# Seven products instead of eight for a sixth pair of the output projection, and an order of pairs of its own for the first block of every stage

## The chip, the cores and the metric

The kernel runs on one core of one Trainium2 chip. The metric is the device time of one execution in microseconds. The kernel before takes 2615.23 us, the median of three runs (2615.0 to 2615.27). Engines are named as in the profile: PE multiplies matrices, PEld loads the stationary operand, DVE, ACT and POOL work on elements, SP only issues DMAs.

## The reference

Two layers of an encoder trunk over 256 tokens of width 4096, everything in float32:

```
for l in range(2):
    h = rmsnorm(x, norm_w[l])
    proj = h @ w_in[l]                      # 4096 -> 11264
    aq, ak, av, ag, rq, rk, rv, rg = split(proj)
    a_out = silu(ag) * gqa_attention(rope(rmsnorm(aq)), rope(rmsnorm(ak)), av)
    r_out = silu(rg) * rmsnorm(bidirectional_retention(rope(rq), rope(rk), rv))
    x = x + concat(a_out, r_out) @ w_out[l] # 4096 -> 4096
return rmsnorm(x, final_norm)
```

Nearly all arithmetic is in the two projections of each layer.

## The kernel before

**Four stages.** Stage 0 is `w_in` of layer 0 (11 blocks of 1024 output columns), stage 1 `w_out` of layer 0 (4 blocks), stages 2 and 3 the same for layer 1. A block multiplies the transposed activations (256 tokens) by 1024 columns of weights. The 4096 input features are cut into 32 tiles of 128, and two neighbouring tiles make a *pair*; a block runs over pairs 0 to 15.

**Three passes for one product.** Weights and activations are split into a high part (rounded to the matmul format) and a low part (the rest), and a product is high by high, high by low, low by high: three matmuls of 512 columns (two at L1559, one at L1569). Pairs 1 and 0 of the very first block take the raw float32 values instead (L1553).

**Eights and sevens.** A pair is a 2 by 2 by 2 problem: two token halves, two feature tiles, two column halves. Done plainly it is eight products (`EIGHT_PRODUCTS`), done in Strassen's way seven (`SEVEN_PRODUCTS`). The table `SEVENS` names the pairs that take seven in each stage, five in every stage of the kernel before. The price of a seven is paid elsewhere. An eight has two weight pages (A and B, 128x1024): each is a load `wraw`, a cast on ACT to `whi`, and a subtraction on DVE to `wlo`. A seven has the same two loads but three and a half pages: A, T and U (128x1024) and half a page B (128x512, `bhi` and `blo`). T and U are sums of the loaded weights, made on DVE in `wsum` by three additions, and need casts and subtractions of their own. On the activations' side a seven needs five sums `xf`, split into `x7h` and `x7l`; an eight only `x8h` and `x8l`.

**Banks.** Eight PSUM banks M1 to M8 hold a block's sums. M1, M5, M7 and M6 serve sevens alone, so they open with the block's first seven and close with its last; outside that window they are lent to attention and retention, whose matmuls stand at L1040 to L1042. At a block's end `combine` adds the banks into `ca` and `cb`. Where DVE is behind, ACT copies a bank to `out` first.

**What sets the order.** The instructions are issued by a planner that runs in the program while it is built: it keeps clocks for PE, DVE and ACT with its own costs (`STEP_V`, `STEP_S`, `LANDING` and others), and between two products it puts in a step of a waiting *task* (rotary, attention, retention, norms, splitting of the next stage's operands) if the weights that PE needs next leave room. The order that comes out is fixed on every engine. Five buffers `whi`, five `wlo`, two each of `bhi` and `blo`, two `wsum` and six `wraw` limit how far DVE and ACT run ahead of PE. Loads of weights are issued by SP; stores, fetches and accumulating DMAs by POOL.

**Between stages.** Activations for the next stage go out transposed to `next_dram` in six chunks of two pairs, are fetched again into `full`, and split; the last two chunks are handed over in SBUF. The residual is added by an accumulating DMA into `ca` and `cb` (L1667 in the last stage).

`GROUPS` cuts the pairs at each seven: the pages of the eights that follow a seven are put between its pages (`TURNS`). Only the first block of all has an order of its own:

```
SEVENS = ((3, 4, 6, 10, 11), (4, 6, 10, 11, 12), (3, 4, 6, 10, 11), (4, 6, 10, 11, 12))
SPREAD = (4, 5, 9, 10, 13)
FIRST_ORDER = [1, 0] + [_p for _p in range(2, NP) if _p not in SEVENS[0]]
...
        for g in FIRST_GROUPS if first_order else GROUPS[stage]:
```

A page can also be made *far*, in a page of the common pool and outside the ring of five: ACT casts it to `fhi`, writes its negative to `flo`, and an accumulating DMA on POOL's queue adds the weights to `flo`, so that DVE has no part in it. `FARS` names such pages; it is empty in the kernel before.

Of the kernel before, what the change touches and what calls it, by code (L numbers as in the profile page):

```python
# [14 lines left out]
ALU = mybir.AluOpType  # L15
# [24 lines left out]
FAR = 1  # L40

STRICT = 9
RELIEF = 0.6
AHEAD = 5
SPARE = 2

HALVES = 2

STEP_V = 1.2
STEP_S = 1.5  # L50

V_FIXED = 0.1
# [3 lines left out]
PASS = 0.3  # L56

LANDING = 9.5
STORE = 5.0
FETCH = 13.0  # L60
FAR_LANDING = 9.0
MARGIN = 0.5

RUSH = 2.5

EARLY = 1.3

ADD_AHEAD = 3.0

NEED = {"ak": 4, "ag": 3, "rk": 5, "rg": 4}  # L70

PE_REST = 1.2

TIGHT_A = 2
TIGHT_B = 9

AT_ONCE = 3

WARM = 20

SPLITS = 1

START = 2

SEVENS = ((3, 4, 6, 10, 11), (4, 6, 10, 11, 12), (3, 4, 6, 10, 11), (4, 6, 10, 11, 12))

EVER = sorted(set(_p for _s in SEVENS for _p in _s))
EIGHTS = [_p for _p in range(NP) if _p not in EVER]
# [9 lines left out]

HOLD = 4

NEAR = 40

LATE = 10

FARS = ((), (), (), ())


AQ, AK, AV, AG, RQ, RK, RVO, RG = 0, 2048, 2560, 3072, 5120, 6144, 7168, 9216
# [65 lines left out]
GROUPS = [  # L174
    ([tuple(range(_s[0]))] if _s[0] else []) + [tuple(range(_a, _b)) for _a, _b in zip(_s, _s[1:] + (NP,))] for _s in SEVENS
]
SPREAD = (4, 5, 9, 10, 13)
FIRST_ORDER = [1, 0] + [_p for _p in range(2, NP) if _p not in SEVENS[0]]
for _i, _p in zip(SPREAD, SEVENS[0]):
    FIRST_ORDER.insert(_i, _p)  # L180
FIRST_GROUPS = []
for _p in FIRST_ORDER:
    if _p in SEVENS[0] or not FIRST_GROUPS:
        FIRST_GROUPS.append(())
    FIRST_GROUPS[-1] += (_p,)
SHARED = ("M1", "M5", "M7", "M6")


# [34 lines left out]
EASY = ("M7",)  # L223


BANK_REST = 0.8
APART = 0.0

TOGETHER = 4
# [52 lines left out]
def hybrid_encoder(  # L282
# [134 lines left out]
    class Weights:  # L417


        def __init__(self):  # L420
            self.pages = []
            for l in range(DEPTH):
                for w, n in ((w_in, N_IN), (w_out, N_OUT2)):
                    for b in range(n):
                        stage = 2 * l + (w is w_out)
                        start = (l, b) == (0, 0) and w is w_in
                        for g in FIRST_GROUPS if start else GROUPS[stage]:
# [337 lines left out]
    def split_operand(c, stage, rest=0.0):  # L765
        v, full[c] = full[c], None
        for k in range(2):
            p = 2 * c + k
            whole = None
            if stage == 0:  # L770
                whole = v.rearrange("p (k i n) -> p k i n", k=2, i=2)[:, k]
                w = v.rearrange("p (k i m a t) -> p k m i a t", k=2, i=2, m=MT, t=BLK)[:, k]
            else:
                w = v.rearrange("p (a m i t) -> p m i a t", a=4, m=MT, t=BLK)[:, :, 2 * k : 2 * k + 2]
            waiting.append(Lane(split_pair(p, w, whole, stage)))
            waiting[-1].pair, waiting[-1].ready = p, now.t + rest
        if stage == 0:
            waiting.sort(key=lambda v: (v.pair in NATIVE and not c, FIRST_ORDER.index(v.pair)))

    def split_late():  # L780
        split_operand(*late.pop(0))
# [77 lines left out]
    force = [False]  # L859

    def take_bank():

# [73 lines left out]
    def running():  # L936
# [4 lines left out]
            one.append(rest)  # L941
        return one

    def advance():

        clear()
# [17 lines left out]
    def tick():  # L964

        weights.low_parts()
# [456 lines left out]
    def lead(stage):  # L1423

        return 8 * SEVENS[stage][0]

    def block(after_pair, phase, then, first_order=False, order=LAST_ORDER, last=None, hurried=False):

# [5 lines left out]
        flat = []  # L1434
        stage = phase - 1
        rush[0] = RUSH if hurried else 0.0
        for g in FIRST_GROUPS if first_order else GROUPS[stage]:
            for slot in slots_of(g, stage, first_order):
                flat += slot
        want[0] = 2  # L1440
# [58 lines left out]
            return a  # L1499

        opens = max(final[b] for b in SHARED)
        after = lead(then - 1) if then else 0

        def end_product(n, name, p, index, k, h):
            g = pages[p, k]
# [70 lines left out]
    def combine(bank, acc, c):  # L1576
# [15 lines left out]
        elif bank in ("M8", "M3", "M2", "M4"):  # L1592
            to = {"M8": cb[:, 1, :], "M3": cb[:, 0, :], "M2": ca[:, 0, :], "M4": ca[:, 1, :]}[bank]
            v = acc[bank]
            if not last_block[0] and ve.until - max(ac.until, now.t) > RELIEF and held[0] + pledged() < PAGES:
                v = page([P, NB], "out")
                ac.copy(v, acc[bank])
                drop()
            ve.tensor_add(to, to, v)

# [250 lines left out]
    for l, L in enumerate(layers):  # L1851
        for bi, (one, _) in enumerate(BLOCKS):
# [10 lines left out]
            c = block(after, 2 * l + 1, 2 * l + 1 + (bi == N_IN - 1), start)  # L1863
            ready = (lambda i=one[1], L=L: i in L.weights) if one[0] == "rg" else None
            tasks.append(Lane(in_task(L, *one, c), need=NEED[one[0]], own=2, gate=ready))
            if one[0] == "ag":
                users.update((v, l, one[1]) for v in "sv")
                tasks.append(Lane(attention_scores(L, one[1]), need=6, gate=lambda g=one[1], L=L: g in L.rs and now.t >= L.kept and near(LATE)))
# [5 lines left out]
        for n in range(N_OUT2):  # L1874
# [19 lines left out]
            else:  # L1894
                if final:
                    turning.append(Turn(2 * l + 2))
                c = block(after, 2 * l + 2, 2 * l + 2 + (n == N_OUT2 - 1), hurried=n == 0)
                tasks.append(Lane(out_tasks(l, n, c), need=4, own=2))


_INS = [
# [46 lines left out]
```

## Time and profile before

| what | before |
|---|---|
| median of 3 runs | 2615.23 us |
| the profiled execution | 2615.02 us |
| its span | 2613.2 us |
| instructions in the span | 33651 |
| HBM read, written | 564.20 MB, 44.04 MB |
| DMA engines, mean busy share, by stage | 0.72, 0.72, 0.71, 0.64 |

The span is that of the program's instructions; 1.8 us of the execution lie outside it. Matmuls are pipelined: the profile gives each of 512 columns about 389 ns, but the next starts long before that, so what one costs is read from the distance of starts. A busy PE is then no proof that PE is at its peak; that has to be seen from starts and waits.

### The profile page before, as it was taken

What the parts mean: (1) busy time and instruction counts of PE and PEld (TensorE: products, weight loads), DVE (VectorE), ACT (ScalarE), POOL (GpSimd) and SP (SyncE); (2) the same over time, 40 slices, a digit from 0 to 9 for tenths busy, and PEclk for the clock granted to TensorE, in tenths of its full rate; (3) what the DMA queues carried; (4) which work ended last, traced back from release to release, by engine and by line L of the source; (5) the groups of instructions that cost most, each with busy time, mean ns of one, the idle gap of its engine ahead of it and who ended that gap; (6) DMA issues with size and microseconds to landing.
All of it is one profiled execution on the core that took longest, in us unless ns stands there. A gap on an engine that the chain in (4) does not pass through costs nothing.

```text
span 2613.2 us, 33651 instructions
## 1 busy us (share of the span) xinstructions
PE 2599.5 (99%) x11650; PEld 2152.7 (82%) x11650; DVE 2283.5 (87%) x2715; ACT 1636.4 (63%) x2376; POOL 238.6 (9%) x368
## 2 busy tenths in 40 slices
PE   9999999999999999999999999999999999999998
PEld 7888888888888888888888888888888888888886
DVE  7998988998888998778998889988988798988777
ACT  7765766666555687555785566675665557765454
POOL 0010211111001000110001101210100010000000
PEclk9999999999999999999999999999999999999999
DMA  7876867876666666786777768777765676667774
GB/s 281 297 246 234 274 224 246 278 230 225 205 212 213 238 209 205 238 274 223 260 228 233 223 233 274 244 232 263 253 225 179 223 232 226 198 205 221 231 243 167
DMA packets 180667, 610.47 MB, mean 234 GB/s; under 512 B 21904, under 2 KB 28560, under 8 KB 180496
## 3 DMA queue, kind: packets, MB, share of 16 engines
q1 hardware_dynamic: 147040, 520.17, 59.4%
q0 software_dynamic: 32736, 87.05, 11.1%
q8 instruction: 91, 1.49, 0.2%
q10 hardware_dynamic: 720, 1.10, 0.1%
q14 instruction: 80, 0.66, 0.1%
HBM read 564.20 MB, written 44.04 MB: 233 GB/s over the span
## 4 chain that ended last, share of the span: by engine, by line
PE 97%; DVE 1%; issue 1%; ACT 1%; DMA 1%; SPq 0%; POOLq 0%; DVEq 0%; POOL 0%; ACTq 0%
PE M L1559 62%; PE M L1569 31%; PE M L1042 1%; PE M L1041 1%; PE M L1040 1%; PE M L1553 0%; DVE wlo L267 0%; DMA wraw<-in_w_in 0%; DMA whole<-in_w_in 0%; ACT whi L267 0%; DVE wsum L267 0%; DVE cb L267 0%; ACT ca L267 0%; DVE ca L267 0%; DVE x7l L267 0%
## 5 line engine op out<-in xcount | busy, mean ns | idle before, releaser
L267 ACT CAST whi<-wraw 128x1024 fp32r<-128x1024 f32 x806 | 835.5, 1047 | 555.8 <-PE M L1559 490.5
L267 DVE TENSOR_TENSOR wlo<-wraw,whi 128x1024 fp32r<-128x1024 f32 x806 | 965.2, 1214 | 129.5 <-ACT whi L267 127.5
L1559 PE MATMUL M<-whi,x8h 128*128 128x512 f32 x2368 | 922.1, 389 | 0.0
L1559 PE MATMUL M<-whi,x8l 128*128 128x512 f32 x2368 | 921.7, 389 | 0.0
L1569 PE MATMUL M<-wlo,x8h 128*128 128x512 f32 x2368 | 679.3, 389 | 0.0
L1559 PEld LDWEIGHTS M<-whi,x8h 128*128 128x128 f32 x2368 | 444.6, 188 | 92.1 <-issue 0.2
L1559 PEld LDWEIGHTS M<-whi,x8l 128*128 128x128 f32 x2368 | 444.6, 188 | 92.0 <-issue 0.2
L1569 PEld LDWEIGHTS M<-wlo,x8h 128*128 128x128 f32 x2368 | 442.8, 188 | 90.8
L267 ACT CAST whi<-wsum 128x1024 fp32r<-128x1024 f32 x300 | 315.5, 1052 | 227.9 <-DVE wsum L267 115.3
L1559 PE MATMUL M<-whi,x7h 128*128 128x512 f32 x1140 | 443.6, 389 | 0.0
L1559 PE MATMUL M<-whi,x7l 128*128 128x512 f32 x1140 | 443.5, 389 | 0.0
L267 DVE TENSOR_TENSOR wlo<-wsum,whi 128x1024 fp32r<-128x1024 f32 x300 | 365.5, 1218 | 27.0 <-ACT whi L267 26.6
L1569 PE MATMUL M<-wlo,x7h 128*128 128x512 f32 x1140 | 341.3, 389 | 0.3 <-DVE wlo L267 0.3
L1569 PEld LDWEIGHTS M<-wlo,x7h 128*128 128x128 f32 x1140 | 213.8, 188 | 45.2 <-DVE wlo L267 0.7
L1559 PEld LDWEIGHTS M<-whi,x7h 128*128 128x128 f32 x1140 | 214.0, 188 | 44.9 <-issue 0.4
L1559 PEld LDWEIGHTS M<-whi,x7l 128*128 128x128 f32 x1140 | 214.0, 188 | 44.4
L267 DVE TENSOR_TENSOR wsum<-wraw 128x1024 f32<-128x1024 f32 x150 | 182.4, 1216 | 1.5 <-DMA wraw<-in_w_in 1.5
L267 DVE TENSOR_TENSOR wsum<-wsum,wraw 128x512 f32<-128x512 f32 x150 | 103.8, 692 | 5.2
L267 DVE TENSOR_TENSOR wsum<-wraw,wsum 128x512 f32<-128x512 f32 x150 | 102.5, 684 | 0.6
L267 DVE TENSOR_TENSOR blo<-wraw,bhi 128x512 fp32r<-128x512 f32 x150 | 102.7, 685 | 0.0
L267 ACT CAST bhi<-wraw 128x512 fp32r<-128x512 f32 x150 | 92.3, 615 | 0.0
L267 DVE TENSOR_TENSOR cb<-cb,M 128x512 f32<-128x512 f32 x85 | 58.0, 682 | 37.5 <-PE M L1569 37.4
(223 smaller groups left out, 1876.6 us busy)
## 6 DMA issues: line engine op xcount, KB each, us to landing
wraw<-in_w_in SPq DMA_DIRECT2D x700, 512.0 KB, 4.5
wraw<-in_w_out SPq DMA_DIRECT2D x256, 512.0 KB, 4.2
full<-next_dram POOLq DMA_DIRECT2D x18, 512.0 KB, 7.4
kv<-kv_dram POOLq DMA_DIRECT2D x16, 512.0 KB, 7.0
p_dram<-room POOLq DMA_DIRECT2D x64, 128.0 KB, 3.6
pT<-p_dram POOLq DMA_DIRECT2D x16, 512.0 KB, 8.6
next_dram<-room POOLq DMA_DIRECT2D x40, 128.0 KB, 4.9
x<-in_x SPq DMA_DIRECT2D x8, 512.0 KB, 6.6
```

The costliest lines, as they stand in the source:

```text
L267: return call(out, *args, **kwargs)
L1040: nc.tensor.matmul(out, a[0], b[0], start=start, stop=False)
L1041: nc.tensor.matmul(out, a[0], b[1], start=False, stop=False)
L1042: nc.tensor.matmul(out, a[1], b[0], start=False, stop=stop)
L1559: nc.tensor.matmul(acc[name], a[i], g.hi[h], start=m == first[name] and not i, stop=False)
L1569: nc.tensor.matmul(acc[name], a, g.lo[h], start=False, stop=m == final[name])
```

## The change

- `SEVENS`: in both `w_out` stages pairs 3, 4, 6, 10, 11 and 13 take seven products (before 4, 6, 10, 11 and 12). The `w_in` stages keep 3, 4, 6, 10 and 11. So pairs 3 and 13 are new among the sevens of `w_out`, and pair 12 is an eight again.
- The first block of every stage has an order of its own, by the tables `SPREAD` to `SPREAD3`. Where the first seven stands in it (`LEADS`) tells the planner how long the four shared banks stay free.
- `FARS` names pair 5 in the last stage: its page B is made far in three of that stage's blocks.
- The planner's numbers: among others `STEP_V` from 1.2 to 2.0 and `PE_REST` from 1.2 to 1.5 (more room is asked for before a task's step is put in), `AT_ONCE` from 3 to 2 tasks, `START` from 2 to 1, `RELIEF` from 0.6 to 1.0.
- `combine` could give an addition to an accumulating DMA, if DVE were late by more than `ADDED`, which is 99.

```
-RELIEF = 0.6
-AHEAD = 5
-SPARE = 2
+RELIEF = 1.0
+ADDED = 99
+AHEAD = 6
+SPARE = 3
...
-STEP_V = 1.2
+STEP_V = 2.0
...
-AT_ONCE = 3
+AT_ONCE = 2
...
-START = 2
+START = 1
-SEVENS = ((3, 4, 6, 10, 11), (4, 6, 10, 11, 12), (3, 4, 6, 10, 11), (4, 6, 10, 11, 12))
+SEVENS = ((3, 4, 6, 10, 11), (3, 4, 6, 10, 11, 13), (3, 4, 6, 10, 11), (3, 4, 6, 10, 11, 13))
...
-FARS = ((), (), (), ())
+FARS = ((), (), (), (5,))
...
+SPREAD = (3, 4, 7, 11, 13)
+SPREAD1 = (3, 6, 8, 10, 11, 13)
+SPREAD2 = (3, 4, 7, 9, 11)
+SPREAD3 = (6, 7, 9, 11, 13, 14)
+def opening_order(stage):
+    spread = (SPREAD, SPREAD1, SPREAD2, SPREAD3)[stage]
+    spread = spread if len(spread) == len(SEVENS[stage]) else SEVENS[stage]
+    order = [_p for _p in ([1, 0] if stage == 0 else [0, 1]) + list(range(2, NP)) if _p not in SEVENS[stage]]
+    for i, p in zip(spread, SEVENS[stage]):
+        order.insert(i, p)
+    return order
...
+FIRST_ORDER = [opening_order(_i) for _i in range(4)]
+FIRST_GROUPS = [grouped(_o, _i) for _i, _o in enumerate(FIRST_ORDER)]
+LEADS = [8 * next(_i for _i, _p in enumerate(_o) if _p in SEVENS[_s]) for _s, _o in enumerate(FIRST_ORDER)]
...
-        for g in FIRST_GROUPS if first_order else GROUPS[stage]:
+        for g in FIRST_GROUPS[stage] if opening else GROUPS[stage]:
...
-        after = lead(then - 1) if then else 0
+        after = 0 if not then else lead(then - 1) if then == phase else LEADS[then - 1]
...
-            if not last_block[0] and ve.until - max(ac.until, now.t) > RELIEF and held[0] + pledged() < PAGES:
+            busy = ve.until - max(ac.until, now.t)
+            if not last_block[0] and busy > RELIEF and held[0] + pledged() < PAGES:
                 v = page([P, NB], "out")
                 ac.copy(v, acc[bank])
+                if busy > ADDED and ac.until < now.t + 2.0:
+                    nc.gpsimd.dma_start(to, v, accum_op=ALU.add)
+                    landing.append(ac.until + LANDING)
+                    return
```

**Where instructions move.** First DVE at the end of the second `w_out` block of layer 0, where the weights of the last pairs are made (`wsum` sums of a seven, `wlo` and `blo` low parts). Before, pair 12 (`wraw_9702`, `wraw_9721`) is the seven and pair 13 (`wraw_9745`, `wraw_9756`) an eight:

```order
L267 TENSOR_TENSOR wlo_9838<-wraw_9702,whi_9837 128x1024
L267 TENSOR_TENSOR wlo_9851<-wraw_9745,whi_9850 128x1024
L267 TENSOR_TENSOR wsum_9862<-wraw_9702,wsum_9835 128x512
L267 TENSOR_TENSOR wsum_9862<-wsum_9862,wraw_9721 128x512
L267 TENSOR_TENSOR wlo_9868<-wsum_9835,whi_9867 128x1024
L267 TENSOR_TENSOR blo_9871<-wraw_9721,bhi_9870 128x512
L267 TENSOR_TENSOR wlo_9884<-wraw_9756,whi_9883 128x1024
L267 TENSOR_TENSOR wlo_9899<-wsum_9862,whi_9898 128x1024
L267 TENSOR_TENSOR wlo_9912<-wraw_9807,whi_9911 128x1024
```

With the change, pair 12 (`wraw_9747` is its second load) is an eight and pair 13 (`wraw_9771`, `wraw_9782`) the seven:

```order
L288 TENSOR_TENSOR wlo_9864<-wraw_9747,whi_9863 128x1024
L288 TENSOR_TENSOR wlo_9879<-wsum_9839,whi_9878 128x1024
L288 TENSOR_TENSOR wsum_9888<-wraw_9771,wraw_9782 128x1024
L288 TENSOR_TENSOR wlo_9891<-wraw_9771,whi_9890 128x1024
L288 TENSOR_TENSOR wlo_9907<-wraw_9842,whi_9906 128x1024
L288 TENSOR_TENSOR wsum_9918<-wraw_9771,wsum_9888 128x512
L288 TENSOR_TENSOR wsum_9918<-wsum_9918,wraw_9782 128x512
L288 TENSOR_TENSOR wlo_9924<-wsum_9888,whi_9923 128x1024
L288 TENSOR_TENSOR blo_9927<-wraw_9782,bhi_9926 128x512
L288 TENSOR_TENSOR wlo_9946<-wraw_9851,whi_9945 128x1024
L288 TENSOR_TENSOR wlo_9961<-wsum_9918,whi_9960 128x1024
```

A seven is seven instructions on DVE where an eight is two. Pair 13 has taken over pair 12's seven, with a page of pair 14 between its own where a page of pair 13 stood; pair 3 is the seven that is added in each `w_out` block.

Second, DVE in the first block of stage 2 (`w_in` of layer 1), around the splitting of the chunks fetched into `full`. Before:

```order
L267 TENSOR_TENSOR x7l_11519<-xf_11520,x7h_11518 128x640
L267 TENSOR_TENSOR wsum_11556<-wraw_11420,wraw_11440 128x1024
L267 TENSOR_TENSOR wlo_11541<-wraw_11395,whi_11540 128x1024
L267 TENSOR_TENSOR wlo_11559<-wraw_11420,whi_11558 128x1024
L267 TENSOR_TENSOR xf_11552<-xf_11552,full_11160 128x128
```

With the change:

```order
L288 TENSOR_TENSOR wlo_11555<-wraw_11425,whi_11554 128x1024
L288 TENSOR_TENSOR x8l_11571<-full_11164,x8h_11570 128x256 x2
L288 TENSOR_TENSOR wsum_11606<-wraw_11463,wraw_11489 128x1024
L288 TENSOR_TENSOR wlo_11591<-wraw_11451,whi_11590 128x1024
L288 TENSOR_TENSOR wlo_11609<-wraw_11463,whi_11608 128x1024
L288 TENSOR_TENSOR xf_11602<-xf_11602,full_11304 128x128
```

Pair 10, a seven, now comes ahead of pair 9, an eight: the split of pair 9 (`x8l_11571`) stands where that of pair 10 (`x7l_11519`) stood, and pair 10's own sums follow later.

Third, ACT in the second block of the last stage, where the far page is made. There is no such row before; with the change:

```order
L288 CAST whi_20726<-wraw_20619 128x1024
L288 COPY out_20735<-M2_19994 128x512
L288 CAST whi_20738<-wraw_20623 128x1024
L288 CAST fhi_20741<-wraw_20635 128x1024
L288 ACTIVATE flo_20742<-fhi_20741 128x1024
L288 CAST whi_20775<-wraw_20675 128x1024
```

On POOL's queue the accumulating DMA that finishes `flo` stands behind the two that add the residual:

```order
L1700 DMA ca_20656<-x2_dram_82 128x1024
L1700 DMA cb_20657<-x2_dram_82 128x1024
L598 DMA flo_20742<-in_w_out 128x1024
L1700 DMA ca_21295<-x2_dram_82 128x1024
L1700 DMA cb_21296<-x2_dram_82 128x1024
```

ACT has two instructions for the far page where it had one cast, DVE has one fewer, and POOL's queue has one DMA more in each of three blocks.

More of the change, by code (lines that the diff above doesn't have):

```diff
@@ L58 @@
 LANDING = 9.5
-STORE = 5.0
+STORE = 7.0
 FETCH = 13.0
-FAR_LANDING = 9.0
-MARGIN = 0.5
-RUSH = 2.5
+FAR_LANDING = 11.0
+MARGIN = 0.0
+RUSH = 1.5
 EARLY = 1.3
-ADD_AHEAD = 3.0
-NEED = {"ak": 4, "ag": 3, "rk": 5, "rg": 4}
-PE_REST = 1.2
+ADD_AHEAD = 1.0
+NEED = {"ak": 5, "ag": 3, "rk": 4, "rg": 4}
+PE_REST = 1.5
 TIGHT_A = 2
 TIGHT_B = 9
-AT_ONCE = 3
+AT_ONCE = 2
 WARM = 20
 SPLITS = 1
-START = 2
-SEVENS = ((3, 4, 6, 10, 11), (4, 6, 10, 11, 12), (3, 4, 6, 10, 11), (4, 6, 10, 11, 12))
+START = 1
+SEVENS = ((3, 4, 6, 10, 11), (3, 4, 6, 10, 11, 13), (3, 4, 6, 10, 11), (3, 4, 6, 10, 11, 13))
 EVER = sorted(set(_p for _s in SEVENS for _p in _s))
@@ L99 @@
 HOLD = 4
-NEAR = 40
-LATE = 10
-FARS = ((), (), (), ())
+NEAR = 30
+LATE = 35
+FARS = ((), (), (), (5,))
 AQ, AK, AV, AG, RQ, RK, RVO, RG = 0, 2048, 2560, 3072, 5120, 6144, 7168, 9216
@@ L176, with grouped @@
 ]
[L177 to L185, printed above, removed]
+SPREAD = (3, 4, 7, 11, 13)
[9 more added lines that the diff above has]
+    return order
+def grouped(order, stage):
+    groups = []
+    for p in order:
+        if p in SEVENS[stage] or not groups:
+            groups.append(())
+        groups[-1] += (p,)
+    return groups
+FIRST_ORDER = [opening_order(_i) for _i in range(4)]
+FIRST_GROUPS = [grouped(_o, _i) for _i, _o in enumerate(FIRST_ORDER)]
+LEADS = [8 * next(_i for _i, _p in enumerate(_o) if _p in SEVENS[_s]) for _s, _o in enumerate(FIRST_ORDER)]
 SHARED = ("M1", "M5", "M7", "M6")
@@ L223 @@
 EASY = ("M7",)
-BANK_REST = 0.8
+BANK_REST = 1.0
 APART = 0.0
@@ L426, in __init__ @@
                         start = (l, b) == (0, 0) and w is w_in
-                        for g in FIRST_GROUPS if start else GROUPS[stage]:
+                        for g in GROUPS[stage] if b else FIRST_GROUPS[stage]:
                             for slot in slots_of(g, stage, start):
@@ L777, in split_operand @@
         if stage == 0:
-            waiting.sort(key=lambda v: (v.pair in NATIVE and not c, FIRST_ORDER.index(v.pair)))
+            waiting.sort(key=lambda v: (v.pair in NATIVE and not c, FIRST_ORDER[0].index(v.pair)))
     def split_late():
@@ L858, in hybrid_encoder @@
     spare, taken, window, want, users, last_block = {}, {}, [0, False, 99], [0], set(), [False]
-    force = [False]
+    force, landing = [False], []
     def take_bank():
@@ L942, in running, with landed @@
         return one
+    def landed():
+        while landing and landing[0] <= now.t:
+            landing.pop(0)
+            drop()
     def advance():
+        landed()
         clear()
@@ L1425, in lead, with block @@
         return 8 * SEVENS[stage][0]
-    def block(after_pair, phase, then, first_order=False, order=LAST_ORDER, last=None, hurried=False):
+    def block(after_pair, phase, then, first_order=False, opening=False, order=LAST_ORDER, last=None, hurried=False):
         flat = []
@@ L1862, in hybrid_encoder @@
                 turning.append(Turn(2 * l + 1))
-            c = block(after, 2 * l + 1, 2 * l + 1 + (bi == N_IN - 1), start)
+            c = block(after, 2 * l + 1, 2 * l + 1 + (bi == N_IN - 1), start, bi == 0)
             ready = (lambda i=one[1], L=L: i in L.weights) if one[0] == "rg" else None
             tasks.append(Lane(in_task(L, *one, c), need=NEED[one[0]], own=2, gate=ready))
+            tasks[-1].ready = max([0.0] + landing)
             if one[0] == "ag":
@@ L1896, in hybrid_encoder @@
                     turning.append(Turn(2 * l + 2))
-                c = block(after, 2 * l + 2, 2 * l + 2 + (n == N_OUT2 - 1), hurried=n == 0)
+                c = block(after, 2 * l + 2, 2 * l + 2 + (n == N_OUT2 - 1), opening=n == 0, hurried=n == 0)
                 tasks.append(Lane(out_tasks(l, n, c), need=4, own=2))
+                tasks[-1].ready = max([0.0] + landing)
 _INS = [
```

1 line of the change is left out of this document (added).

## The prediction

> **What bounds the kernel now.** I read the page first: the shares of the engines and the chain of work that ended last.
>
> ```profile
> span 2613.2 us, 33651 instructions
> PE 2599.5 (99%) x11650; PEld 2152.7 (82%) x11650; DVE 2283.5 (87%) x2715; ACT 1636.4 (63%) x2376; POOL 238.6 (9%) x368
> PE 97%; DVE 1%; issue 1%; ACT 1%; DMA 1%; SPq 0%; POOLq 0%; DVEq 0%; POOL 0%; ACTq 0%
> PE M L1559 62%; PE M L1569 31%; PE M L1042 1%; PE M L1041 1%; PE M L1040 1%; PE M L1553 0%; DVE wlo L267 0%; DMA wraw<-in_w_in 0%; DMA whole<-in_w_in 0%; ACT whi L267 0%; DVE wsum L267 0%; DVE cb L267 0%; ACT ca L267 0%; DVE ca L267 0%; DVE x7l L267 0%
> ```
>
> PE is 97% of the chain, nearly all of it the projections' products. A busy share of 99% proves little, since a matmul is shown longer than its share of the pipe, so next I read the waits of PE (total, times, longest).
>
> ```profile
> PE M L1812 <- DVE half L267: 1.1, 1, 1.1
> PE M L1569 <- DVE wlo L267: 0.3, 1, 0.3
> PE M L1553 <- DMA whole<-in_w_in: 0.3, 1, 0.3
> ```
>
> Two of the three waits belong to the start. In the whole run PE waits visibly once for weights. For the distance of starts, the chain in order of time (start, length, what):
>
> ```profile
> 366.49 1.81 PE M L1559 x8
> ...
> 901.80 1.15 DVE wlo L267
> 902.96 7.98 DMA wraw<-in_w_in
> ...
> 943.63 1.23 DVE wlo L267
> 944.91 0.73 PE M L1569 x2
> ```
>
> Eight products in a row take 1.81 us, so one costs 0.2265 us. So the kernel stands at PE's floor: what PE does not compute is time won, as long as the others keep up; and little is to be won by better ordering. The one wait for weights, at 944.9 us, has a history: at 902.96 us a load of weights took 7.98 us, after it DVE ran without rest, and 40 us later PE had used up the weights made ahead. In PE's timeline:
>
> ```profile
> 944.22 0.39 PE L1559 MATMUL M<-whi,x7l 128*128 128x512 f32 x1
> 944.91 0.73 PE L1569 MATMUL M<-wlo,x7h 128*128 128x512 f32 x2 [0.29 <-DVE wlo L267]
> ```
>
> The starts lie 0.69 us apart instead of 0.227: PE lost 0.46 us there.
>
> **The change part by part.** *Products.* A pair that turns from eight products to seven saves one product, three matmuls. `w_out` has one such pair more in each of 4 blocks of 2 layers, `w_in` none: 24 matmuls of 512 columns, and PE's order is 24 rows shorter. 24 x 0.2265 = 5.44 us off the path.
>
> The Trainium skill has a rule that would make this smaller: "TensorE: Matmul & The Clock Gate", section "Back-to-back issue gap", gives about 131 ns a matmul of 512 columns in a sustained stream of weight loads and matmuls. By it the saving would be an estimated 3.1 us. The trace does not agree: its stream stands at 227 ns throughout, so the measurement decides.
>
> *DVE.* From its timeline, the weights of a seven:
>
> ```profile
> 937.83 1.22 DVE L267 TENSOR_TENSOR wsum<-wraw 128x1024 f32<-128x1024 f32 x1
> 938.96 1.22 DVE L267 TENSOR_TENSOR wlo<-wraw,whi 128x1024 fp32r<-128x1024 f32 x1
> ...
> 942.30 0.68 DVE L267 TENSOR_TENSOR wsum<-wraw,wsum 128x512 f32<-128x512 f32 x1
> 943.02 0.69 DVE L267 TENSOR_TENSOR wsum<-wsum,wraw 128x512 f32<-128x512 f32 x1
> 943.63 1.22 DVE L267 TENSOR_TENSOR wlo<-wsum,whi 128x1024 fp32r<-128x1024 f32 x1
> 944.77 0.68 DVE L267 TENSOR_TENSOR blo<-wraw,bhi 128x512 fp32r<-128x512 f32 x1
> 945.37 1.22 DVE L267 TENSOR_TENSOR wlo<-wraw,whi 128x1024 fp32r<-128x1024 f32 x1
> ```
>
> By their starts: the first sum 1.13, the two half sums 0.72 and 0.61, a large low part 1.14, the half one 0.60. A seven has three sums, three large low parts and a half one, 6.48 us; an eight two large low parts, 2.28. So 4.20 us more a block, 16.8 us a `w_out` stage; the three far pages give 3 x 1.14 = 3.4 us back in the last one. Is there room? Busy time by stage (stages 0 to 3, then the tail):
>
> ```profile
> 0.00:968.00 968.00, 966.25 (x4327) 796.53 (x4328) 861.68 (x1054) 622.38 (x929) 98.43 (x157) 1.00 0.72 242
> 968.00:1306.00 338.00, 338.00 (x1504) 280.30 (x1504) 286.20 (x325) 208.82 (x290) 29.97 (x44) 1.00 0.72 238
> 1306.00:2263.00 957.00, 957.00 (x4320) 795.67 (x4319) 852.20 (x1018) 607.96 (x897) 101.31 (x157) 1.00 0.71 232
> 2263.00:2601.00 338.00, 338.00 (x1504) 280.22 (x1502) 279.38 (x311) 194.53 (x258) 8.34 (x9) 1.00 0.64 209
> 2601.00:2613.20 12.20, 0.26 (x2) 0.00 (x0) 4.01 (x10) 2.67 (x5) 0.55 (x1) 0.62 0.65 241
> ```
>
> The third busy column is DVE: 85% and 83% in the `w_out` stages. With the addition it is (286.2 + 16.8) / 335.3 = 90% and (279.4 + 13.4) / 335.3 = 87%. The `w_in` stages run at 89% (861.68 of 968, 852.20 of 957) and lose half a microsecond. So on the mean the work hides behind PE. If it did not, 33.6 - 3.4 = 30 us would come onto the path, the upper bound. The granted clock is 1.00 in all four stages.
>
> *ACT.* A cast and a half more a block, an instruction more for each of three far pages, and 16 more bank copies `out`; the page has `whi` at 1047 ns and the tile's view the copy:
>
> ```profile
> L267 ACT CAST whi<-wraw 128x1024 fp32r<-128x1024 f32 x806 | 835.5, 1047 | 555.8 <-PE M L1559 490.5
> L267 ACT COPY out<-M x10: 589/589/589, 89.1 to 2002.6; 128x512 f32<-128x512 f32 x10
> L267 DVE TENSOR_TENSOR cb<-cb,out x5: 684/685/693, 91.3 to 2001.6; 128x512 f32<-128x512 f32 x5
> ```
>
> That is some 8 x 1.6 + 3 x 1.0 + 16 x 0.59 = 25 us over the whole run, on an engine that is idle for 37% of it: nothing. The addition on DVE that follows costs 685 ns, as from the bank.
>
> *The far page.* In three blocks PE takes `flo` from an accumulating DMA. No row of before shows one from the weights; the nearest are the residual's, which stand just ahead of it on POOL's queue:
>
> ```profile
> 2350.38 0.69 DVE L267 TENSOR_TENSOR ca<-ca,M 128x512 f32<-128x512 f32 x1 [0.67 <-PE M L1569]
> ...
> 2351.53 0.90 POOL L1667 DMA_DIRECT2D ca<-x_dram  x1 [67.46 <-DVE ca L267]
> 2352.13 1.20 POOL L1667 DMA_DIRECT2D cb<-x_dram  x1
> ```
>
> and, of the DMA issues (count, size, median time to landing):
>
> ```profile
> ca<-x_dram POOLq DMA_DIRECT2D x3, 512.0 KB, 6.7
> cb<-x_dram POOLq DMA_DIRECT2D x3, 512.0 KB, 11.0
> wraw<-in_w_out SPq DMA_DIRECT2D x256, 512.0 KB, 4.2
> wraw<-in_w_in SPq DMA_DIRECT2D x700, 512.0 KB, 4.5
> ```
>
> The second of a pair lands 11.0 us after its issue, 4.3 later than the first; a third behind them should land 4.3 later again, some 16 us after the pair's issue (bounds: 7, alone on the queue, and 20). In the changed order PE takes `flo` 125 products, 28 us, after the last product of the block before; the pair is issued under 2 us after that product, as the first two rows show. That leaves 6 us at the worse bound. No cost.
>
> *The openings.* Two rows of the start, of DVE and of PE:
>
> ```profile
> 11.72 1.23 DVE L267 TENSOR_TENSOR wlo<-wraw,whi 128x1024 fp32r<-128x1024 f32 x1 [3.11 <-ACT whi L267]
> ...
> 31.13 0.39 PE L1559 MATMUL M<-whi,x7h 128*128 128x512 f32 x1
> ```
>
> The second is the first product of the first seven. With the change, two pages of eights now stand ahead of the first seven instead of four, so PE wants it 24 products, 5.4 us, sooner: about 25.7 us instead of 31.1. Laying DVE's rows one behind another from that first `wlo` at 11.72 us, the seven's first low part is ready at about 20 us and its activations at 21. In the next ten microseconds the margin shrinks to about 1 us. I take no loss, 1 us as the bound. In `w_in` of layer 1 it is closer. Counting DVE's rows by the starts above, from the first block's first low part to the one that PE takes 47 us later: before 41.0 us of work for 45.1 us of products, now 46.3 us for 46.9. The windows over that place have DVE at 41.91 of 45 already:
>
> ```profile
> 895.00:945.00 50.00, 49.70 (x220) 40.61 (x218) 46.35 (x65) 37.75 (x63) 3.68 (x5) 1.00 0.61 210
> 1307.00:1352.00 45.00, 45.00 (x201) 37.24 (x199) 41.91 (x56) 39.73 (x73) 4.34 (x5) 1.00 0.76 239
> ```
>
> At 93% no wait came of it, while 46.35 of 50 with a late load in it ended in the 0.46 us. At 99% a late load can't be made up. Bounds: 0 to 3.5 us (7.98 less the usual 4.5). I take 0.5 us for all openings together, since the five buffers are full when the stage begins and no load need be late.
>
> *The sum.* The tail from 2601 us on has the same rows in the same order, so it stays. 2615.02, the profiled execution, less 5.44 is 2609.58; half a microsecond of new waits against the 0.46 that the new order may be rid of leaves 2609.6. The median of the runs lies 0.2 us above that execution, so **2609.7 us**.
>
> **The rivals.** *Short waits (R1).* DVE falls behind once or twice at the openings, and PE pays 1 to 6 us: 2611 to 2616, in the middle 2612. For it: the 99% above, and that tasks now wait for more room and come in fewer at a time, so that they bunch later. Against it: 89% over two whole `w_in` stages with one wait.
>
> *Loads collide and DVE never recovers (R2, the other side).* The fetches of `full` on POOL's queue delay a load of weights by 3.5 us as at 902.96. It decides where DVE has no rest to make it up: at the last block of both `w_in` stages and at the three later openings. Five places at 3.5 us are 17.5: 2627. It is slower by more than can be told from the fourth place on (2609.6 + 14.0 = 2623.6). Against it: the same collision cost 0.46 us before, and the DMA engines are busy 0.64 to 0.76.
>
> The Trainium skill, "DMA: Bandwidth & Descriptors", section "Issuing engines are not separate DMA queues", says that DMAs of all queues share the 16 engines and interleave. By that rule the far page's DMA delays loads of weights too; with the 7.98 us beside a median of 4.5 the trace agrees.
>
> *The saving does not come (R3).* If PE were held by something else in `w_out`, fewer products would change nothing: 2615. PE's 338.00 of 338 there without a wait speak against it; I give it no chance of its own beside R1.
>
> **How the numbers follow.** Forecast 0.60 (2608.8 to 2610.4), R1 with R3 0.31, R2 0.09. A measurement here can tell 0.2%, 5.2 us, from no change: the bound is 2610.0, just above the forecast. Of the forecast's 0.60 some 0.06 lie over it. So faster 0.54, within 0.2% 0.37, slower 0.09. The range goes from 2608.7 (all waits after the start gone) to 2613.0, which takes in the nearer two thirds of R1.
>
> **What would show it.** Right: 24 matmuls fewer, starts still 0.227 us apart, DVE near 90% in the `w_out` stages, no row of PE waiting for DVE over half a microsecond, the tail 12 us. R1: waits of PE for `wlo` or `x7l` within 50 us of a stage's opening. R2: the same with loads of 8 us ahead of them, at four places. A wait of PE for DMA `flo` would prove the far page's margin wrong. The forecast is wrong if the waits new in the trace sum to over 1 us.

## The result and the profile after

The changed kernel takes **2610.07 us** (median of 17 runs, 2609.26 to 2611.09), the kernel before 2615.06 us beside it (17 runs, 2614.40 to 2615.54). The ratio is 0.9981, with a 95% interval from 0.9974 to 0.9988: faster by 5.0 us, 0.19%. The profiled execution took 2609.94 us with a span of 2608.2, before 2615.02 and 2613.2.

The page of the changed kernel: span, busy time of the engines, and the shares of the chain that ended last.

```profile
span 2608.2 us, 33718 instructions
PE 2594.3 (99%) x11626; PEld 2148.0 (82%) x11626; DVE 2313.5 (89%) x2760; ACT 1662.6 (64%) x2413; POOL 238.3 (9%) x371
PE 96%; DVE 2%; issue 1%; ACT 1%; DMA 0%; SPq 0%; DVEq 0%; POOLq 0%; POOL 0%; ACTq 0%
```

PE has 24 matmuls fewer. DVE has 30.0 us more work (2313.5 against 2283.5), ACT 26.2 us more, and the time still fell: PE is the bound as before, and the others' new work lies beside it. The waits of PE (total, times, longest):

```profile
PE M L1845 <- DVE half L288: 1.1, 1, 1.1
PE M L1581 <- DMA whole<-in_w_in: 0.7, 2, 0.4
PE M L1597 <- DVE wlo L288: 0.2, 1, 0.2
```

The first two lines belong to the start, as they did before. The third names one wait for weights. The stages' windows (length; busy time of PE, PEld, DVE, ACT and POOL; granted clock, DMA share, GB/s):

```profile
0.00:968.00 968.00, 966.00 (x4327) 796.16 (x4328) 861.89 (x1053) 620.47 (x924) 97.71 (x157) 1.00 0.73 242
968.00:1303.30 335.30, 335.30 (x1492) 278.11 (x1491) 301.26 (x347) 221.01 (x310) 28.88 (x44) 1.00 0.73 239
1303.30:2260.30 957.00, 956.95 (x4318) 795.29 (x4317) 853.64 (x1019) 608.68 (x895) 100.49 (x157) 1.00 0.71 233
2260.30:2595.70 335.40, 335.40 (x1492) 278.18 (x1491) 292.74 (x333) 209.76 (x282) 10.66 (x12) 1.00 0.67 215
```

Both `w_out` stages are 2.7 us shorter, twelve matmuls each at 0.2265 us, and PE is busy in every microsecond of them. DVE stands at 301.26 / 335.3 = 90% and 292.74 / 335.4 = 87% there. The small loss lies elsewhere. PE's timeline in the last `w_in` block of layer 0:

```profile
939.96 0.39 PE L1587 MATMUL M<-whi,x7l 128*128 128x512 f32 x1
940.45 0.73 PE L1597 MATMUL M<-wlo,x7h 128*128 128x512 f32 x2
...
944.44 0.39 PE L1587 MATMUL M<-whi,x7l 128*128 128x512 f32 x1
944.98 0.74 PE L1597 MATMUL M<-wlo,x7h 128*128 128x512 f32 x2 [0.16 <-DVE wlo L288]
```

The starts lie 0.49 and 0.54 us apart where a stream has 0.227: 0.26 and 0.31 us lost, and 0.11 in the matmul after each, which is why the two-matmul rows show 0.73 instead of the usual 0.62. The list of waits shows only one of these places, because it counts idle time after a modelled end that lies later than the next possible start; the distance of starts shows both. With a third such place at 2238.3 us, the lost starts sum to 1.14 us, against 0.57 at the one such place before; two more of 0.07 us stand in both traces. So 5.44 - 0.57 = 4.87 us is what PE should have gained; its last matmul starts at 2595.99 us, before at 2600.87, which is 4.88.

### The profile page after: what moved, and what is told of

Read it like the earlier page. It is cut to its first block, busy times and chain, and to the rows that moved or that the text cites. A ratio compares the mean times of both kernels' runs of the same rounds, so it can differ in the third digit from the quotient of the medians.

```text
span 2608.2 us, 33718 instructions
## 1 busy us (share of the span) xinstructions
PE 2594.3 (99%) x11626; PEld 2148.0 (82%) x11626; DVE 2313.5 (89%) x2760; ACT 1662.6 (64%) x2413; POOL 238.3 (9%) x371
## 4 chain that ended last, share of the span: by engine, by line
PE 96%; DVE 2%; issue 1%; ACT 1%; DMA 0%; SPq 0%; DVEq 0%; POOLq 0%; POOL 0%; ACTq 0%
PE M L1587 62%; PE M L1597 31%; PE M L1070 1%; PE M L1069 1%; PE M L1068 1%; DVE wlo L288 1%; PE M L1581 0%; DVE wsum L288 0%; ACT whi L288 0%; DMA whole<-in_w_in 0%; ACT ca L288 0%; DVE ca L288 0%; DVE cb L288 0%; DVE x8l L288 0%; DVE xf L288 0%
## 5 line engine op out<-in xcount | busy, mean ns | idle before, releaser
L288 ACT CAST whi<-wraw 128x1024 fp32r<-128x1024 f32 (+1 forms) x795 | 823.9, 1046 | 501.9 <-PE M L1587 434.8
L288 DVE TENSOR_TENSOR wlo<-wraw,whi 128x1024 fp32r<-128x1024 f32 (+1 forms) x795 | 951.2, 1213 | 107.8 <-ACT whi L288 105.8
L1597 PE MATMUL M<-wlo,x8h 128*128 128x512 f32 x2356 | 672.1, 389 | 0.0
L288 ACT CAST whi<-wsum 128x1024 fp32r<-128x1024 f32 x316 | 332.4, 1052 | 262.6 <-DVE wsum L288 138.2
L1587 PE MATMUL M<-whi,x7h 128*128 128x512 f32 x1124 | 437.4, 389 | 0.0
L1587 PE MATMUL M<-whi,x7l 128*128 128x512 f32 x1124 | 437.3, 389 | 0.0
L288 DVE TENSOR_TENSOR wlo<-wsum,whi 128x1024 fp32r<-128x1024 f32 x316 | 384.8, 1218 | 33.4 <-ACT whi L288 31.9
L288 DVE TENSOR_TENSOR wsum<-wraw 128x1024 f32<-128x1024 f32 x158 | 192.1, 1216 | 1.5 <-DMA wraw<-in_w_in 1.2
L288 DVE TENSOR_TENSOR wsum<-wsum,wraw 128x512 f32<-128x512 f32 x158 | 109.4, 692 | 5.5
L288 DVE TENSOR_TENSOR cb<-cb,M 128x512 f32<-128x512 f32 x74 | 50.4, 681 | 23.8 <-PE M L1597 23.8
```

The source lines that it names most:

```text
L288: return call(out, *args, **kwargs)
L1587: nc.tensor.matmul(acc[name], a[i], g.hi[h], start=m == first[name] and not i, stop=False)
L1597: nc.tensor.matmul(acc[name], a, g.lo[h], start=False, stop=m == final[name])
```

## The experiments

Ten more kernels were run. The kernel before ran beside each on the same chip (medians 2615.14 to 2615.18 us). An interval is about 0.09% wide to each side, 2.4 us, so steps of 1 us are read from the traces and not from the ratio alone.

**Is it the products? Five sevens again.**

```
-SEVENS = ((3, 4, 6, 10, 11), (3, 4, 6, 10, 11, 13), (3, 4, 6, 10, 11), (3, 4, 6, 10, 11, 13))
+SEVENS = ((3, 4, 6, 10, 11),) * 4
...
-SPREAD1 = (3, 6, 8, 10, 11, 13)
+SPREAD1 = (3, 6, 8, 10, 11)
...
-SPREAD3 = (6, 7, 9, 11, 13, 14)
+SPREAD3 = (6, 7, 9, 11, 13)
```

> The changed kernel with w_out back at five seven-product pairs (3, 4, 6, 10, 11); its numbers for the planner, its own openings and its far page stay. 24 matmuls more than the changed kernel. Theory (the gain is the products, 24 x 0.2265 us = 5.44 us, and the rest of the edit costs some 0.5 us of new waits): 2615.5 us, level with before or 0.2 to 0.5 us over it. Rival (the gain comes from the order and the planner's numbers): about 2610 us, as the changed kernel.

Measured: 2615.46 us, ratio to before 1.0002 (0.9993 to 1.0011). Everything else of the change stayed, and the gain was gone to the last half microsecond. Its `w_out` stages are 338.00 us long again. New orders and numbers alone bring nothing.

**Are the products enough? Only the table of sevens in the kernel before.**

```
-SEVENS = ((3, 4, 6, 10, 11), (4, 6, 10, 11, 12), (3, 4, 6, 10, 11), (4, 6, 10, 11, 12))
+SEVENS = ((3, 4, 6, 10, 11), (3, 4, 6, 10, 11, 13), (3, 4, 6, 10, 11), (3, 4, 6, 10, 11, 13))
```

> The kernel before with one line changed: w_out's seven-product pairs become 3, 4, 6, 10, 11, 13. The planner's numbers and the order of the openings stay as before. Theory (products alone): 24 matmuls fewer, 2609.6 us, give or take 0.5 us of waits. Rival 1 (the other edits are what lets the loads of VectorE hide): PE waits for wlo or x7l at the openings of the w_out stages, 2611 to 2616 us. Rival 2 (six pairs without the planner's numbers never fit): over 2616 us.

Measured: 2617.45 us, ratio 1.0010 (1.0001 to 1.0019): slower than before, though PE has the same 24 matmuls fewer. The theory fell, and so did rival 1, whose waits for `wlo` or `x7l` at the openings do not appear. The time is that of rival 2, but its reason, the planner's numbers, is refuted below. The waits of PE in this run:

```profile
PE M L1559 <- DVE ca L267: 4.8, 2, 2.4
```

Twice, 24 us into each `w_out` stage, PE waits for DVE's work on `ca`, not for weights. Counted by starts the two places cost 4.04 and 4.07 us, and -5.44 + 8.11 and 0.3 of other waits is the 3.0 us by which its span of 2616.2 exceeds that of before. So the saving is real and something else in the change protects it: the opening orders, the planner's numbers, or both.

**Which part protects it? The two halves apart.** First the changed kernel with plain openings in the three later stages:

```
-                        for g in GROUPS[stage] if b else FIRST_GROUPS[stage]:
+                        for g in FIRST_GROUPS[stage] if start else GROUPS[stage]:
...
-        for g in FIRST_GROUPS[stage] if opening else GROUPS[stage]:
+        for g in FIRST_GROUPS[stage] if first_order else GROUPS[stage]:
```

(and `LEADS` as eight times each stage's first seven).

> The changed kernel with an opening order of its own in the very first block alone; the first blocks of the other three stages take their pairs in the plain order, as before. Its planner's numbers, six pairs and far page stay. In the run six_alone PE stood 4.0 us behind VectorE's bank addition (ca) 24 us into each w_out stage. Theory O (the opening orders take that stall away): it is back, about 4 us in each w_out stage, 2617 to 2619 us. Theory N (the planner's numbers take it away): 2610 us, no wait for ca.

Then the changed kernel with the planner's numbers of before:

```
-RELIEF = 1.0
+RELIEF = 0.6
-STEP_V = 2.0
+STEP_V = 1.2
-AT_ONCE = 2
+AT_ONCE = 3
...
```

> The changed kernel with the planner's numbers of before (the sixteen constants from RELIEF to BANK_REST and NEED); the opening orders, six pairs and far page stay. Theory N (the numbers take the stall of six_alone away): the waits for ca 24 us into the w_out stages are back, some 4 us each, 2617 to 2619 us. Theory O (the opening orders do): 2610 us, give or take 1 us of other waits. If both are needed it is over 2612 us in this run and in plain_open.

Measured: 2618.24 us with plain openings, ratio 1.0012 (1.0003 to 1.0021), and 2611.08 us with the old numbers, ratio 0.9984 (0.9975 to 0.9993). Theory O holds: the openings' order is worth some 8 us, the numbers some 1 us (by the trace, 1.1 us of small losses in the very first block, between 31 and 35 us; the medians' difference alone would not prove it). The stall in PE's timeline with plain openings:

```profile
988.61 0.39 PE L1587 MATMUL M<-whi,x7l 128*128 128x512 f32 x1
991.41 0.50 PE L1587 MATMUL M<-whi,x7h 128*128 128x512 f32 x1 [2.40 <-DVE ca L288]
```

and DVE in the same run, just before:

```profile
987.35 1.22 DVE L288 TENSOR_TENSOR wlo<-wraw,whi 128x1024 fp32r<-128x1024 f32 x1
...
989.42 0.16 DVE L288 TENSOR_SCALAR rst<-rst 128x2 f32<-128x2 f32 x1
990.48 0.88 DVE L288 SCALAR_TENSOR_TENSOR ca<-M,rst,ca 128x256 f32<-128x256 f32 x2 [0.89 <-POOL rst L432]
```

This is the end of a task of the layer's retention. Its result stands in a bank (`ca<-M`), and DVE takes it out into `ca` with the factor `rst`, for which it waits 0.89 us for a step of POOL. Only then does PE start the seven's fourth product. The trace does not name the bank; by the kernel's table that product goes to M7, a shared one. In the changed kernel the same instructions come 2.9 us sooner on DVE:

```profile
986.53 0.15 DVE L288 TENSOR_SCALAR rst<-rst 128x2 f32<-128x2 f32 x1
...
987.58 0.88 DVE L288 SCALAR_TENSOR_TENSOR ca<-M,rst,ca 128x256 f32<-128x256 f32 x2
```

and PE has other work: after pair 3's first two products it goes on with products of pair 5, an eight, until 991.5 us. In the plain order pairs 3 and 4, both sevens, follow one another, so that pair 3 stands in a group by itself with no page of an eight between its own, and the four of its seven products that go to shared banks (M1, M5, M7 and M6) come close together. Before the change this did not arise: the first seven of `w_out` was pair 4, with an eight behind it.

**How much of the order is needed? One exchange.**

```
-SPREAD1 = (3, 6, 8, 10, 11, 13)
+SPREAD1 = (3, 5, 6, 10, 11, 13)
...
-SPREAD3 = (6, 7, 9, 11, 13, 14)
+SPREAD3 = (3, 5, 6, 10, 11, 13)
```

> The changed kernel, but with the opening orders of both w_out stages cut to one exchange against the plain order: 0, 1, 2, 3, 5, 4, 6, 7, and so on in order, so that one pair of eight products (5) lies between the first two seven-product pairs (3 and 4). Theory S (the stall of plain_open comes from two seven-product pairs in a row while VectorE still holds banks of the last w_in block's result): the one exchange takes it away, 2610.1 us within 0.5. Rival (the whole order is needed, since VectorE's extra work has to be spread over the block): PE waits for ca or wlo over 1 us in the first w_out block, 2612 to 2618 us.

Measured: 2613.36 us, ratio 0.9993 (0.9984 to 1.0002). The time is in the rival's range, but the mechanism is half of each. The wait for `ca` is gone, so a single eight between the first two sevens does what theory S says. Counted by starts, the 4.28 and 4.27 us that PE lost at the two stalls go, and 1.38 us come in at each `w_out` opening, in small pieces some 10 us further on. In the medians this is worth 4.9 of the 8.2 us between 2618.24 and 2610.07. The longest of the new pieces in PE's timeline:

```profile
1002.68 0.61 PE L1597 MATMUL M<-wlo,x7h 128*128 128x512 f32 x2
1003.47 0.50 PE L1587 MATMUL M<-whi,x7h 128*128 128x512 f32 x1 [0.18 <-ACT whi L288]
```

Here it is the weights of sevens that come a little late, where pairs 4 and 6 follow one another. That fits the rival's mechanism, the spreading of the extra work over the block, but no run separates it. The order of the change has neither loss.

**The far page.**

```
-FARS = ((), (), (), (5,))
+FARS = ((), (), (), ())
```

> The changed kernel without the far page: pair 5 of the last stage is added by VectorE instead of by a transfer that accumulates. VectorE gets about 3.4 us of work more in the last stage, which it has room for by the 87% there. Expected: no change, 2610.1 us within 0.5. Rival (the far page carries part of the gain): over 2611 us, with PE waiting for VectorE in the last stage.

Measured: 2610.18 us, ratio 0.9981 (0.9972 to 0.9990). No difference in time to the change, and no wait of PE in the last stage. The far page carries nothing of the gain that could be measured.

**The losses that are left: where do they come from?** In the last `w_in` block of each layer four fetches of `full` are issued by POOL one behind another, in layer 0 at 900.7 us, right after a slow step (1.54 us) that they were queued behind. Only the issuing engine was changed, to ScalarE; PE and DVE have the same instructions in the same order.

```
-            nc.gpsimd.dma_start(full[c], next_dram[c])
+            nc.scalar.dma_start(full[c], next_dram[c])
```

> The changed kernel with the fetch of the next stage's input (full<-next_dram) issued by ScalarE in place of GpSimd, where four fetches wait behind one slow operation and are let go together at 900.7 and 2194.5 us. Theory A (those late fetches crowd VectorE's splits into the last w_in block of each layer): the waits at 940, 945 and 2238 us (1.1 us in all) go, 2609.0 us. Theory B (VectorE is too full in those blocks whatever the fetches do): the waits stay within 0.3 us of what they are, 2610 us. Rival (ScalarE's own work is held up by the issues): some 2611 us, with waits of PE for ScalarE.

Measured: 2609.03 us (2608.51 to 2609.37), ratio to before 0.9977 (0.9968 to 0.9986). The median is 1.0 us below that of the change; the intervals of the two overlap, so the trace has to bear the claim. ACT, POOL and DVE in the changed kernel:

```profile
905.79 1.05 ACT L288 CAST whi<-wraw 128x1024 fp32r<-128x1024 f32 x1
910.92 1.05 ACT L288 CAST whi<-wraw 128x1024 fp32r<-128x1024 f32 x1 [4.08 <-DMA wraw<-in_w_in]
...
900.69 2.18 POOL L853 DMA_DIRECT2D full<-next_dram  x4
...
919.36 1.22 DVE L288 TENSOR_TENSOR wlo<-wraw,whi 128x1024 fp32r<-128x1024 f32 x1 [0.34 <-ACT whi L288]
922.11 1.23 DVE L288 TENSOR_TENSOR wlo<-wsum,whi 128x1024 fp32r<-128x1024 f32 x1 [1.52 <-ACT whi L288]
```

and with ScalarE as the issuer:

```profile
901.63 0.33 ACTq L853 DMA_DIRECT2D full<-next_dram  x1
...
906.48 1.05 ACT L288 CAST whi<-wraw 128x1024 fp32r<-128x1024 f32 x1
908.06 1.05 ACT L288 CAST whi<-wraw 128x1024 fp32r<-128x1024 f32 x1 [0.53 <-DMA wraw<-in_w_in]
```

In ACT's order the fetches are spread: two are issued at 901.6 and 904.9 us, the third at 920.7. With four in 2.2 us, the load of weights issued at 902.79 us lands after 8.04 us; with ScalarE's issues the same load lands after 4.48, and ACT's wait for it falls from 4.08 to 0.53. In the changed kernel ACT splits that page late, then has its copies and casts in a row, and DVE stands idle for ACT between 914 and 925 us. The windows show it (same columns as above), first for the kernel before, then with the change, then with ScalarE's issues:

```profile
912.00:926.00 14.00, 14.00 (x63) 11.60 (x62) 10.49 (x17) 13.70 (x28) 0.00 (x0) 1.00 0.65 227
912.00:926.00 14.00, 14.00 (x64) 11.58 (x63) 10.57 (x16) 13.70 (x26) 0.00 (x0) 1.00 0.66 226
912.00:926.00 14.00, 14.00 (x64) 11.59 (x63) 13.18 (x19) 13.38 (x23) 0.00 (x0) 1.00 0.69 238
```

DVE, the third busy column, is nearly full on both sides of that stretch, so with POOL's issues it comes to the same instructions at 940 us 2.2 us later, and PE has used up what was made ahead. With ScalarE all three places of loss (940, 945, 2238 us) are gone; one new wait of 0.33 us appears at 608 us. The sum of lost starts after the kernel's own start falls from 1.28 to 0.58 us, counting everything over 0.04.

The size of this gain is not firm. Up to the last stage the run without the far page has the same instructions as the change on PE, DVE and ACT, and its lost starts sum to 0.72 us in place of 1.28: executions differ by that much. Theory A is shown for the layer-0 place, step by step and in every trace: the kernel before, the change and the six runs above lose 0.40 to 0.85 us around 940 and 945 us, the kernels with ScalarE's issues (this one and the next) lose nothing there. For 2238 us it is not shown. The same wait of ACT stands there (3.61 us at 2204.3, none with ScalarE), but the run without the far page waits 3.27 us too and PE loses nothing.

The same edit in the kernel before:

> The kernel before with the fetch of the next stage's input issued by ScalarE in place of GpSimd, as in the run fetch_act. Theory A (the four fetches let go together at 900.9 us make a weight load of w_in late, ScalarE's split of it then VectorE's): before's one wait of 0.46 us at 944.9 us goes, 2614.6 us. Rival (the gain of fetch_act has to do with the rest of the change): 2615.1 us or more.

Measured: 2614.40 us, ratio 0.9997 (0.9989 to 1.0006). The loss of 0.46 us at 944.9 us is gone from its trace, and the span is 0.9 us shorter. So the flaw is older than the change. Whether the change made it dearer the traces can't tell, since executions of the same instructions differ as much.

**Does it go further? Six sevens in `w_in` too.**

```
-SEVENS = ((3, 4, 6, 10, 11), (3, 4, 6, 10, 11, 13), (3, 4, 6, 10, 11), (3, 4, 6, 10, 11, 13))
+SEVENS = ((3, 4, 6, 10, 11, 13),) * 4
...
-SPREAD = (3, 4, 7, 11, 13)
+SPREAD = (3, 4, 7, 10, 11, 13)
...
-SPREAD2 = (3, 4, 7, 9, 11)
+SPREAD2 = (3, 4, 7, 9, 11, 13)
```

> The changed kernel with six seven-product pairs in the w_in stages too, so 66 matmuls fewer still: 66 x 0.2265 = 14.95 us. VectorE's load in the w_in stages goes from 861.9 of 968.0 us (89%) to about (861.9 + 11 x 4.2) / (968.0 - 7.5) = 94.5%. Theory (VectorE hides until it is nearly full): 2595 to 2598 us. Rival (the waits in the last w_in blocks show that VectorE is at its limit there, and the waits grow with each block): over 2605 us, and the rows of PE waiting for VectorE's whi, wlo or half sum to 10 us or more.

And in the second layer's `w_in` alone, with ScalarE's fetches:

```
-SEVENS = ((3, 4, 6, 10, 11), (3, 4, 6, 10, 11, 13), (3, 4, 6, 10, 11), (3, 4, 6, 10, 11, 13))
+SEVENS = ((3, 4, 6, 10, 11), (3, 4, 6, 10, 11, 13), (3, 4, 6, 10, 11, 13), (3, 4, 6, 10, 11, 13))
...
-SPREAD2 = (3, 4, 7, 9, 11)
+SPREAD2 = (3, 4, 7, 9, 11, 13)
...
-            nc.gpsimd.dma_start(full[c], next_dram[c])
+            nc.scalar.dma_start(full[c], next_dram[c])
```

> The changed kernel with the fetch issued by ScalarE (as in fetch_act, 2609.03 us) and six seven-product pairs in the w_in stage of the second layer too: 33 matmuls fewer, 33 x 0.2265 = 7.47 us, and VectorE's load there from 853.6 / 957.0 = 89% to (853.6 + 46.2) / 949.5 = 94.8%. Theory (the run win_six was held up in its first layer and carried the delay on; VectorE at 95% can still hide): 2601.6 to 2604 us. Rival (at 95% VectorE no longer catches up between blocks; win_six lost 35 us of PE in this stage): 2620 us or more, PE waiting for VectorE and ScalarE in the second w_in stage in nearly every block.

Measured: 2775.89 us, ratio 1.0614 (1.0599 to 1.0628), and 2686.18 us, ratio 1.0269 (1.0255 to 1.0284). What these two compute is not the reference; which part of it differs was not found, so their times are those of a near relative and settle nothing about a sound version. Both theories missed. The rivals have the sign, but not the reason: in the first run PE's waits for `wlo`, `whi` and `half` sum to 2.6 us, not 10 or more, and in the second PE waits long at three places of the edited stage (near 1745, 1840 and 1920 to 1950 us), not in nearly every block. Counted by starts, the second run's `w_in` stage with the edit loses 35 us and the unedited `w_out` stage behind it 47. The three largest waits of PE in the whole of it:

```profile
PE M L1587 <- ACT x8h L288: 19.3, 5, 9.0
PE M L1587 <- DVE sgT L288: 10.1, 3, 4.4
PE M L1587 <- DVE x8l L288: 7.3, 4, 4.4
```

PE does not wait for the weights that a seven makes dear. In the edited stage it waits above all for tasks that empty lent banks (`sgT<-M`, 10.1 us, and `pr<-M`, 7.2), from the end of that stage on for activations (`x8h`, `x8l`). A last seven at pair 13 instead of 11 leaves the shared banks to the tasks for a shorter time in each block, and `w_in` is where most of the tasks are. That would explain it; it was not tested.

## Why the prediction was right, point by point

- *Products.* Right. 24 fewer, the stream still at 0.227 us a start, 2.7 us off each `w_out` stage, and the run with five sevens gives all of it back. The measured 4.9 us goes with the trace's own spacing. The smaller saving, an estimated 3.1 us by the Trainium skill's figure ("TensorE: Matmul & The Clock Gate", section "Back-to-back issue gap"), did not come.
- *DVE.* Right to a per cent: forecast 90% and 87%, measured 90% and 87%. That a mean below 100% suffices is only half the story: in the run with the plain order, DVE's total is nearly the same (2315.4 us) and the kernel is slower than before. The mean said that the work fits; the order decided whether it came in time. "Little is to be won by better ordering" holds for five sevens, as the first run shows, and not for six.
- *ACT.* Forecast 25 us more, measured 26.2, and no cost; the 16 more bank copies came (26 against 10).
- *The far page.* Forecast to land 16 us after the pair's issue, bounds 7 and 20. The tile's view of the changed kernel has issues and matmuls, and the time to landing (least, median, most):

```profile
L1597 PE MATMUL M<-flo,x8h x12: 389/389/389, 2375.7 to 2542.3; 128*128 128x512 f32 x12
L598 POOL DMA_DIRECT2D flo<-in_w_out x3: 844/852/1376, 2351.5 to 2517.1; - x3
DMA to landing us min/median/max: 13.4/13.9/15.0
```

  Counted from the pair's issue the three land after 16.3, 16.4 and 16.1 us. From the page's own issue to its first use there are 24.2 us (2351.5 to 2375.7) in the first block, 15.0 of them until it lands. No wait, and without the page no change: the size was right, and the page brings nothing here.
- *The openings.* The bottom line was right, no loss at any of them (the first seven's product, wanted at about 25.7 us, starts at 25.44 without a wait), but the step looked at the wrong danger. It costed the new orders as a risk of late weights (0.5 us, up to 3.5), with nothing on the other side. The runs show that without them the saving turns into a loss of 3 us. In the plain order nearly all of that is a bank that DVE empties late, 4.28 us at each of two stalls, a wait that the prediction did not have among its terms. With that gone and the order otherwise plain, 1.38 us a stage of late weights come up, the danger that it did name. The first could have been looked for in the trace of before: that task ends at about 989 us there, 21 us into the stage, and pairs 3 and 4 side by side ask for shared banks.
- *The waits.* "Half a microsecond of new waits against the 0.46 that the new order may be rid of": the old one stayed and the sum grew by 0.57. All of it lies in the last `w_in` blocks, none at an opening. So the term's place was wrong, and that half a microsecond came out near its size was luck: the run without the far page, with the same instructions there, has 0.01 us more than before in place of 0.57. The growth is 0.53 us over the net 0.04 of the forecast, and covers the 0.4 us between 2609.7 and 2610.07; it stays under the bound of 1 us that the prediction set.
- *The rivals.* R1 asked for waits within 50 us of a stage's opening: none came, and the median lies within the forecast's own range (to 2610.4). R2's collision did happen, with a load 3.6 us late at both last `w_in` blocks, and cost tenths of a microsecond, not 3.5 us a place: weights made ahead paid for the rest. The prediction misread one thing there: after the late load DVE did not run without rest, it stood idle for ACT, in the kernel before too (busy for 10.49 of 14 us from 912 to 926). R3 fell with the first experiment.
- *The tail* is 12.2 us from PE's last start, before 12.3.

## What to carry to other kernels

When an edit moves work from the bounding engine to one that is 87% busy, look past the mean: find the first place after the edit where two of the dearer items follow one another, and what else (a bank, a slot, a factor from a slow engine) they need there. Test an edit of several parts by taking each away on its own: here one line alone was slower than the kernel before, the rest without that line was worth nothing, and only that line and the orders together gained. And look at who issues DMAs: here transfers queued behind a slow instruction were let go in one burst, and the burst was paid for 40 us later.

## What was not expected of the hardware

A short stall of PE costs more than its length. Granted clock in the run with plain openings, by windows around the stall (same columns as above):

```profile
988.60:991.40 2.80, 0.40 (x2) 0.00 (x0) 1.87 (x8) 0.72 (x1) 0.71 (x1) 1.00 0.58 186
991.40:993.50 2.10, 2.09 (x8) 1.54 (x9) 1.19 (x4) 0.00 (x0) 0.70 (x1) 0.81 0.01 2
993.50:996.00 2.50, 2.50 (x7) 1.97 (x7) 2.50 (x4) 1.47 (x4) 0.00 (x0) 0.50 0.00 0
996.00:1000.00 4.00, 4.00 (x19) 3.25 (x18) 3.54 (x5) 3.89 (x8) 0.00 (x0) 0.99 0.40 131
```

The same after the stall in the run with the table of sevens alone:

```profile
991.88:994.00 2.12, 2.12 (x5) 1.73 (x6) 1.21 (x4) 0.00 (x0) 0.70 (x1) 0.50 0.00 0
```

With plain openings PE stood for 2.4 us, started again at full clock, and 1.3 us later the clock fell to 0.50 for 3.41 us; in the other run the clock was at 0.50 as soon as PE started again. Of the 4.28 us lost, 2.57 are the stall and 1.7 the slow matmuls after it; all four such stalls, two in each of two kernels, cost 4.0 to 4.3 us each. The waits of 0.2 to 0.5 us elsewhere left the clock alone.

The clock records of the traces show when it falls. Every length between two changes of the clock is a whole multiple of 3.413 us (from the first rise to the first fall it is 986.45 us, 289 of them, in both runs above). So the clock is set on a beat that does not start with the stall. Counted in these beats, over the four runs in which the clock fell midway (the two above and the two with six sevens in `w_in`), PE stood (from a shown end to the next start) for 0.8 to 1.94 us of a beat at full clock 29 times, and the next beat kept 1.00; it stood for 1.95 us or more 33 times, and the next beat had 0.50. A stall that two beats share can thus go free: in the run with six sevens in the second `w_in` a wait of 2.02 us that ended at 2376.43 us did.

The Trainium skill, "TensorE: Matmul & The Clock Gate", section "Why this matters for your kernels", asks for no idle gaps above some 3 us between bursts; here a gap of 2.4 us was enough each time, so a bound of 3 us is too generous for this kernel.
